# Two quads of modulation weights moved from the S5 stage to the DeltaNet stage, and the low parts of weights made by adding DMA transfers

## The chip, the cores and the metric

One core of a Trainium2 chip runs the whole program. TensorE (PE) multiplies, VectorE (DVE) and ScalarE (ACT) work on elements, SyncE (SP) issues most DMA transfers, and GpSimd (POOL) does almost nothing before the change. The metric is the device time of one execution in microseconds (us).

## The reference, cut to what matters

The program is one inference step of a trunk of two layers on 384 tokens (128 of context, 256 latent) of width 1024, in fp32.

```python
for l in range(2):
    m = silu(cond) @ w_mod[l] + b_mod[l]            # 1024 x 6144: six parts
    sh1, sc1, g1, sh2, sc2, g2 = split(m, 6)
    h = rms(x) * (1 + sc1) + sh1
    out = ab_mix(h) if l == 0 else cd_mix(h)
    x = x + g1 * out
    x = x + g2 * ffn(rms(x) * (1 + sc2) + sh2)
# ab_mix: p = h @ w_in_ab; an S5 state space on one part, gated
#   DeltaNet on the others, both as forward and backward scans; @ w_out_ab
# cd_mix: p = h @ w_in_cd; windowed and differential attention; @ w_out_cd
# ffn:    (silu(conv(h @ up_a)) * (h @ up_b)) @ down
```

## The kernel before, in words

All products are kept near fp32 accuracy by splitting both sides into a high part and a low part, with three matmuls for each pair of tiles: high by low, low by high, high by high (`mm3`, L1119 to L1121, and L1355 to L1357 for the attention layer's projection). Weights come in units of 128x1024 elements (512 KB). `load_unit` (L265) loads one unit into a tile `raw` (three buffers) through SP's DMA queue; ACT rounds it to the high part `wh` (L271), and DVE subtracts that from `raw` to give the low part `wl` (L272). `wh` and `wl` have four buffers each.

The modulation weights `w_mod` are not split. `mod_quad(l, q)` (L987) multiplies two of a layer's six parts: it brings 16 loads of 512 KB straight into tiles that it borrows from the tags `raw`, `wh` and `wl` (SP, L1001), and issues 64 matmuls of 32x512, four at a time on four column groups (L1004), then copies the sums (ACT, L1014), turns them into columns (PE, L1017) and adds the bias (DVE). Quad (0,0) is needed at the very start, (0,1) and (0,2) by the first layer's output projection and feed-forward part, the three quads of layer 1 by the second layer.

The stages of the profiled execution are: setup of norms and S5 tables, until about 86 us; four S5 octets beside the input projection of the first layer (`project`, tiles `pj`, `su`, `sy`, `mm`), until about 222 us; four DeltaNet cores (`gdn_core`, tiles whose names start with g), until about 351 us; the output projection (`out_half`), until 392 us; the feed-forward part, until 681 us; attention (`layer_cd`), until 880 us; the second feed-forward part to the end. In the setup, `s5kd` (L518) stores small S5 tables to DRAM and `s5tp` (L527) reads them back in another layout; the S5 matmuls of line 605 wait for that.

The quads (0,1) and (0,2) run as a side generator: after each unit that `project` multiplies it does one step of a quad, two loads and eight matmuls, with tiles of the tag `raw` alone and a PSUM bank of its own, `mq`. The quads of layer 1 follow the DeltaNet cores 0, 1 and 2, with all eleven buffers and the bank `mod`.

The order in which each engine issues its instructions is not that of the code: a list scheduler (`Order`, with its own table of costs) orders all instructions by their longest path and writes the result to each engine's in-order queue. The hardware then follows these queues.

Of the kernel before, what the change touches and what calls it, by code (L numbers as in the profile page):

```python
# [4 lines left out]

# [1 line left out]

# [209 lines left out]
class Trunk:  # L217
    def __init__(self, ctx, tc, I, O):
        self.ctx, self.tc, self.nc, self.I, self.O = ctx, tc, tc.nc, I, O
        self.tiles = {}  # L220
        nc = self.nc
        self.cp = ctx.enter_context(tc.tile_pool(name="cp", bufs=1))
        self.wp = ctx.enter_context(tc.tile_pool(name="wp", bufs=3))
        self.n = 0
        self.nraw = 0
        self.side = iter(())
        self.cst = self.cp.tile([P, NCST], F32, name="cst")
        self.sml = self.cp.tile([P, NSML], F32, name="sml")
        for tile_, name, first in ((self.sml, "sml", NSML_FIRST), (self.cst, "cst", NCST_FIRST)):
            nc.sync.dma_start(tile_[:, :first], I[name][:, :first])  # L230
            nc.sync.dma_start(tile_[:, first:], I[name][:, first:])
# [31 lines left out]


    def load_unit(self, src, cols=1024):  # L265
        nc = self.nc
        raw = self.t(self.wp, [P, 1024], "raw", bufs=3)
        nc.sync.dma_start(raw[:, :cols], src)
        wh = self.t(self.wp, [P, 1024], "wh", F32R, bufs=4)
        wl = self.t(self.wp, [P, 1024], "wl", F32R, bufs=4)  # L270
        nc.scalar.copy(wh[:, :cols], raw[:, :cols])  # L271
        nc.vector.tensor_sub(wl[:, :cols], raw[:, :cols], wh[:, :cols].bitcast(F32))  # L272
        return wh, wl


# [850 lines left out]
    def project(self, srcs, xh, xl, together=None, tag="mm", n=T):  # L1126


        if together:
            out = [self.bank(tag, [P, n]) for tag in together]  # L1130
            todo = [(p_, *w) for p_, w in zip(out, srcs)]
            for k in range(KD):
                sl = slice(P * k, P * k + P)
                for p_, wh, wl in todo:
                    self.mm3(p_, (wh[:, sl], wl[:, sl]), (xh[k], xl[k]), k == 0, k == KD - 1)
            return out
        out = []
        for src in srcs:
            wh, wl = self.load_unit(src)
            p_ = self.bank(tag, [P, n])  # L1140
            out.append(p_)
            for k in range(KD):
                sl = slice(P * k, P * k + P)
                self.mm3(p_, (wh[:, sl], wl[:, sl]), (xh[k], xl[k]), k == 0, k == KD - 1)
            next(self.side, None)
        return out

    def residual(self, l, gate, n, ps):
# [5 lines left out]

    def ffn(self, l):
        nc, v, t, tc = self.nc, self.nc.vector, self.t, self.tc
        with tc.tile_pool(name=f"fp{l}", bufs=2, reuse_waits="tile") as pool:
            up = [self.I["ffn_up"][l, j, i] for j in range(KF) for i in range(2)]
            pre = self.preload(up[:4])
            hh, hl = self.raw_mod(pool, l, 1)  # L1160
            rb = t(pool, [P, T], "nrb", bufs=1)
            nc.scalar.copy(rb, self.norm_stats(self.np))
            gh, gl = [], []
            cw = self.s("fcw").rearrange("p (l f k) -> p l f k", l=2, k=3)
            cb = self.s("fcb").rearrange("p (l f) -> p l f", l=2)
            first = self.project(pre, hh, hl, together=["mm"] * 4, n=T + 2)
            for j in range(KF):
                pab = first[2 * j:2 * j + 2] if j < 2 else self.project(up[2 * j:2 * j + 2], hh, hl, n=T + 2)
                z = []
                for i, ps in enumerate(pab):  # L1170
                    sh = t(pool, [P, 2], f"fsh{i}")
                    nc.scalar.copy(sh, ps[:, T:])
                    z.append((t(pool, [P, T], f"fz{i}"), sh))
                    v.tensor_mul(z[i][0], ps[:, 0:T], rb)  # L1174
                (pa, sa), (pb, sb) = z
                for c, a, b in SEGS:
                    nc.scalar.activation(pa[:, a:b], pa[:, a:b], AF.Identity, bias=sa[:, c:c + 1])  # L1177
                w = cw[:, l, j]
                y = t(pool, [P, T], "fy")
                nc.scalar.activation(y, pa, AF.Identity, scale=w[:, 1:2], bias=cb[:, l, j:j + 1])  # L1180
                for _, a, b in SEGS:
                    v.scalar_tensor_tensor(y[:, a + 1:b], pa[:, a:b - 1], w[:, 0:1], y[:, a + 1:b],  # L1182
                                           ALU.mult, ALU.add)
                    v.scalar_tensor_tensor(y[:, a:b - 1], pa[:, a + 1:b], w[:, 2:3], y[:, a:b - 1],
                                           ALU.mult, ALU.add)
                s = t(pool, [P, T], "fs")
                nc.scalar.activation(s, y, AF.Silu)  # L1187
                for c, a, b in SEGS:
                    v.scalar_tensor_tensor(s[:, a:b], pb[:, a:b], sb[:, c:c + 1], s[:, a:b], ALU.add, ALU.mult)  # L1189
                a_, b_ = t(pool, [P, T], "fgh", F32R, bufs=KF), t(pool, [P, T], "fgl", F32R, bufs=KF)  # L1190
                nc.scalar.copy(a_, s)
                v.tensor_sub(b_, s, a_.bitcast(F32))
                gh.append(a_)
                gl.append(b_)
            for n in range(KD):
                ps = self.mm([P, T])
                k = 0
                for at in range(0, KF, 8):
                    cnt = min(8, KF - at)
                    wh, wl = self.load_unit(self.I["ffn_down"][l, n][:, at * P:(at + cnt) * P], cols=cnt * P)  # L1200
                    for i in range(cnt):
                        sl = slice(P * i, P * i + P)
                        self.mm3(ps, (wh[:, sl], wl[:, sl]), (gh[k], gl[k]), k == 0, k == KF - 1)
                        k += 1
                self.residual(l, 5, n, ps)


    def layer_ab(self):
        nc, v, t, tc, I = self.nc, self.nc.vector, self.t, self.tc, self.I
        uT, heads = [], []  # L1210
        with ExitStack() as outer:
            sk = outer.enter_context(tc.tile_pool(name="sk", bufs=1, side="right"))
            with self.banks("ps0", mm=2, pj=2, su=1, sy=1, mod=1, mq=1), \
                    tc.tile_pool(name="sp", bufs=1, reuse_waits="tile") as sp:
                with tc.tile_pool(name="st", bufs=1, reuse_waits="tile") as st:
                    self.load_x(st)
# [10 lines left out]
                with tc.tile_pool(name="sw", bufs=1, reuse_waits="tile") as sw:  # L1227
# [2 lines left out]
                        nc.scalar.copy(u, ps)  # L1230
                        uT.append(u)
                    U = [self.s5_inputs(sw, u) for u in uT]
                    self.side = chain(*(self.mod_quad(0, q, tags=("raw",), bank="mq") for q in (1, 2)))
                    for o in range(4):
                        self.s5_octet(sw, o, uT[o], U[o], R[o])
                        if o + 2 < 4:
# [5 lines left out]
                        if o < 3:  # L1242
                            heads.append(self.gdn_head(kq, sw, o, hh, hl, "pj", "gth"))
                    self.s5_states(sw)
                    for _ in self.side:
                        pass
            self.load_x(self.ctx.enter_context(tc.tile_pool(name="xp", bufs=1, reuse_waits="tile")))
            with self.banks("ps1", g1=2, g2=1, g3=2, g4=2, mod=1), \
                    tc.tile_pool(name="gp", bufs=1, reuse_waits="tile") as gp:
                self.gdn_setup(gp)  # L1250
                heads.append(self.gdn_head(kq, gp, 3, hh, hl, "mod", "gcv"))
                self.gelu2(gp, uT[3], "go", 1)
                self.s5_gate(gp, uT)
                ya = [self.split(u, 0.25) for u in uT]
                for h in range(4):
                    self.gdn_core(gp, h, *heads[h])
                    if h < 3:
                        list(self.mod_quad(1, h))
                self.out_half(0, I["w_out_ab"], 0, ya, ("mod",))
                self.out_half(0, I["w_out_ab"], 1, [self.split(x[3]) for x in heads], AB_BANKS)  # L1260

# [67 lines left out]


    def layer_cd(self):
        nc, v, t, tc, I = self.nc, self.nc.vector, self.t, self.tc, self.I
        ident = self.c("ident")
        with tc.tile_pool(name="dpl", bufs=1, reuse_waits="tile") as pool:
# [267 lines left out]

STARTED, BEHIND, WAITED = -1, 0, 1
DMA_RATE, DMA_FIXED = 350.0, 2000.0
PE_GHZ, PE_TICK, PE_WARM = 2.4, 4096 / 1.2, 1210.0


class Order:
# [156 lines left out]
    def duration(self, k):  # L1765
        inst, e = self.insts[k], self.engine[k]
        if self.dma[k]:
            return 450.0
        size = lambda a: math.prod(tuple(x)[1] for x in list(a.bass_ap.ap)[1:])
        outs, ins = ([a for a in ops if hasattr(a, "bass_ap")] for ops in (inst.outs, inst.ins))  # L1770
        if e == "pe":
# [12 lines left out]
    def latency(self, a, b, kind):  # L1784
        if "pools" in (self.engine[a], self.engine[b]):
            return 0.0
        if self.dma[a]:
            return DMA_FIXED + self.bytes[a] / DMA_RATE
        return 0.0 if kind == BEHIND else LATENCY.get((self.engine[a], self.engine[b]), 100)

    def paths(self):
# [27 lines left out]
    def schedule(self):  # L1819
# [12 lines left out]
        def place(k, s):  # L1832
# [17 lines left out]
            if self.dma[k]:  # L1850
                dma_end = max(s + 1500, dma_end) + self.bytes[k] / DMA_RATE
            for b, kind in self.succ[k]:
                f = s + 1 if kind == STARTED else dma_end + 500 if self.dma[k] else end + self.latency(k, b, kind)
                when[b] = max(when[b], f)
                left[b] -= 1
                if not left[b]:
# [78 lines left out]
```

## Time and profile before

| what | value |
|---|---|
| median of 3 runs | 1180.38 us (1179.24 to 1181.22) |
| profiled execution | 1175.78 us, of which the trace spans 1174.0 us |
| mean granted clock of PE | 0.974 |
| PE busy | 1118.2 us (95%) |
| DVE busy | 831.2 us (71%) |
| ACT busy | 582.5 us (50%) |
| DMA moved | 160.85 MB, mean 137 GB/s |

A busy share is a mean over stages with different limits. The profiled execution is 4.6 us under the median; sums are made against it.

### The profile page before, as it was taken

How to read it: one execution, taken by the hardware profiler on the slowest of the kernel's cores; microseconds unless marked ns; L12 is line 12 of the kernel's file. 1: busy time of each engine (PE TensorE's matmuls, PEld its weight loads, DVE VectorE, ACT ScalarE, POOL GpSimd, SP SyncE). 2: the span in 40 equal slices, each digit the busy share in tenths (PEclk: the TensorE clock that was granted, in tenths of full speed). 3: DMA queues.
4: the chain of work that ended last, by engine and by line, in shares of the span. 5: the costliest groups of instructions: out<-in, count | busy, mean ns of one | idle time of the engine just before them, and what ended most of it. 6: DMA issues, size and time to landing. Idle time of an engine off the chain costs nothing.

```text
span 1174.0 us, 20291 instructions
## 1 busy us (share of the span) xinstructions
PE 1118.2 (95%) x7699; PEld 970.2 (83%) x7699; DVE 831.2 (71%) x2097; ACT 582.5 (50%) x1301; POOL 2.9 (0%) x15
## 2 busy tenths in 40 slices
PE   4899999999999999999999979999998999999998
PEld 1587676786559999999999968556788999999998
DVE  7987798689777877777744378786867877676432
ACT  5667463557554555555533234545445655554221
POOL 0000000000000000000000000000000000000000
PEclk9699998999999999999999989999999999999999
DMA  9344474428953234334344323212013343333541
GB/s 372 138 127 149 147 245 164 174 91 301 337 197 127 90 112 140 114 120 143 104 130 130 122 100 125 81 55 81 30 44 115 119 130 122 126 124 103 161 134 55
DMA packets 50737, 160.85 MB, mean 137 GB/s; under 512 B 8272, under 2 KB 12240, under 8 KB 50384
## 3 DMA queue, kind: packets, MB, share of 16 engines
q1 hardware_dynamic: 49200, 154.72, 39.5%
q10 hardware_dynamic: 1440, 4.85, 1.1%
q8 instruction: 60, 0.98, 0.3%
q14 instruction: 37, 0.30, 0.1%
HBM read 156.53 MB, written 3.01 MB: 136 GB/s over the span
## 4 chain that ended last, share of the span: by engine, by line
PE 85%; DVE 8%; DMA 2%; ACT 2%; issue 1%; ACTq 0%; DVEq 0%; SPq 0%
PE mm L1120 16%; PE mm L1121 16%; PE mm L1119 16%; PE mod L1004 3%; PE mm L1355 2%; PE mm L1356 2%; PE mm L1357 2%; PE sc L1477 1%; DVE wl L272 1%; PE mod L1119 1%; PE pj L1121 1%; PE mod L1120 1%; PE mq L1004 1%; PE pj L1120 1%; PE pj L1119 1%
## 5 line engine op out<-in xcount | busy, mean ns | idle before, releaser
L272 DVE TENSOR_TENSOR wl<-raw,wh 128x1024 fp32r<-128x1024 f32 (+2 forms) x193 | 227.0, 1194 | 118.1 <-ACT wh L271 117.8
L271 ACT CAST wh<-raw 128x1024 fp32r<-128x1024 f32 (+2 forms) x193 | 194.0, 1026 | 232.3 <-PE mm L1121 166.6
L1119 PE MATMUL mm<-ah,wl 128*128 128x386 f32 (+1 forms) x732 | 234.8, 343 | 5.2 <-DVE xt L1151 3.6
L1120 PE MATMUL mm<-al,wh 128*128 128x386 f32 (+1 forms) x732 | 233.9, 342 | 2.1 <-DVE al L1097 1.6
L1121 PE MATMUL mm<-ah,wh 128*128 128x386 f32 (+1 forms) x732 | 233.6, 341 | 0.0
L1119 PEld LDWEIGHTS mm<-ah,wl 128*128 128x128 f32 x732 | 138.2, 191 | 6.9 <-ACT wh L271 3.0
L1120 PEld LDWEIGHTS mm<-al,wh 128*128 128x128 f32 x732 | 138.5, 191 | 3.0 <-DVE al L1097 2.1
L1121 PEld LDWEIGHTS mm<-ah,wh 128*128 128x128 f32 x732 | 138.5, 191 | 0.0
L1121 PE MATMUL mm<-fgh,wh 128*128 128x384 f32 x352 | 107.2, 339 | 0.0
L1120 PE MATMUL mm<-fgl,wh 128*128 128x384 f32 x352 | 106.9, 338 | 0.0
L1119 PE MATMUL mm<-fgh,wl 128*128 128x384 f32 x352 | 106.9, 338 | 0.0
L1177 ACT ACTIVATE fz<-fz,fsh 128x128 f32<-128x128 f32 x88 | 35.5, 448 | 67.2 <-DVE fz L1174 67.2
L1119 PEld LDWEIGHTS mm<-fgh,wl 128*128 128x128 f32 x352 | 65.4, 188 | 0.0
L1120 PEld LDWEIGHTS mm<-fgl,wh 128*128 128x128 f32 x352 | 65.2, 188 | 0.0
L1121 PEld LDWEIGHTS mm<-fgh,wh 128*128 128x128 f32 x352 | 65.1, 188 | 0.0
L1151 DVE SCALAR_TENSOR_TENSOR xt<-mm,mod,xt 128x128 f32<-128x128 f32 (+1 forms) x38 | 14.0, 412 | 62.5 <-PE mm L1121 62.5
L1174 DVE TENSOR_TENSOR fz<-mm,nrb 128x384 f32<-128x384 f32 x88 | 45.9, 549 | 0.2
L1182 DVE SCALAR_TENSOR_TENSOR fy<-fz,sml,fy 128x127 f32<-128x127 f32 x88 | 36.4, 413 | 12.8 <-ACT fy L1180 12.1
L1119 PE MATMUL pj<-ah,wl 128*128 128x384 f32 x112 | 39.4, 353 | 2.3 <-DVE wl L272 2.3
L1189 DVE SCALAR_TENSOR_TENSOR fs<-fz,fsh,fs 128x128 f32<-128x128 f32 x88 | 32.7, 413 | 12.4 <-ACT fs L1187 11.2
L1355 PE MATMUL mm<-wh,al 128*128 128x512 f32 (+1 forms) x120 | 38.8, 396 | 2.0 <-DVE al L1074 2.0
L1121 PE MATMUL pj<-ah,wh 128*128 128x384 f32 x112 | 39.9, 356 | 0.0
(661 smaller groups left out, 2163.5 us busy)
## 6 DMA issues: line engine op xcount, KB each, us to landing
raw<-in_ffn_up_dram SPq DMA_DIRECT2D x88, 512.0 KB, 3.4
raw<-in_w_mod_dram SPq DMA_DIRECT2D x54, 512.0 KB, 4.6
raw<-in_ffn_down_dram SPq DMA_DIRECT2D x32, 512.0 KB, 4.5
wh<-in_w_mod_dram SPq DMA_DIRECT2D x21, 512.0 KB, 6.3
wl<-in_w_mod_dram SPq DMA_DIRECT2D x21, 512.0 KB, 6.1
raw<-in_w_in_ab_dram SPq DMA_DIRECT2D x20, 512.0 KB, 3.6
raw<-in_w_in_cd_dram SPq DMA_DIRECT2D x18, 512.0 KB, 3.3
raw<-in_ffn_down_dram SPq DMA_DIRECT2D x16, 384.0 KB, 3.2
```

Of the source, the lines that this page charges most:

```text
L271: nc.scalar.copy(wh[:, :cols], raw[:, :cols])
L272: nc.vector.tensor_sub(wl[:, :cols], raw[:, :cols], wh[:, :cols].bitcast(F32))
L1004: nc.tensor.matmul(pr[32 * n:32 * n + 32], self.sc[:, k, 30 - 2 * b:62 - 2 * b], raws[n // 2][:, 512 * (n % 2):512 * (n % 2) + 512], start ...
L1119: nc.tensor.matmul(out, wl, xh, start=first, stop=False)
L1120: nc.tensor.matmul(out, wh, xl, start=False, stop=False)
L1121: nc.tensor.matmul(out, wh, xh, start=False, stop=last)
L1174: v.tensor_mul(z[i][0], ps[:, 0:T], rb)
L1177: nc.scalar.activation(pa[:, a:b], pa[:, a:b], AF.Identity, bias=sa[:, c:c + 1])
L1182: v.scalar_tensor_tensor(y[:, a + 1:b], pa[:, a:b - 1], w[:, 0:1], y[:, a + 1:b], ALU.mult, ALU.add)
L1189: v.scalar_tensor_tensor(s[:, a:b], pb[:, a:b], sb[:, c:c + 1], s[:, a:b], ALU.add, ALU.mult)
L1355: nc.tensor.matmul(ps[c], hl[k][:, ts_], wh[:, sl], start=k == 0, stop=False)
L1356: nc.tensor.matmul(ps[c], hh[k][:, ts_], wl[:, sl], start=False, stop=False)
```

## The change

The quads (0,1) and (0,2) leave the S5 stage. After core 0 of the DeltaNet stage come quads (0,1) and (0,2), after core 1 quads (1,0) and (1,1), after core 2 quad (1,2). The bank of `mq` goes to `su`.

Outside the feed-forward parts `load_unit` makes the low part in another way: ACT writes the rounded and negated unit into `wl`, and a DMA transfer issued by POOL reads the same unit once more from DRAM and adds it onto `wl`. That holds for 57 units (20 of `w_in_ab` and a small one of `w_ab`, 2 of `w_glu`, 8 of `w_out_ab`, 18 of `w_in_cd`, 8 of `w_out_cd`). The units of both feed-forward parts keep the subtraction on DVE. The scheduler gets a latency and an issue cost for the adding transfers.

```diff
     def load_unit(self, src, cols=1024):
...
         nc.scalar.copy(wh[:, :cols], raw[:, :cols])
-        nc.vector.tensor_sub(wl[:, :cols], raw[:, :cols], wh[:, :cols].bitcast(F32))
+        if self.added:
+            nc.scalar.mul(wl[:, :cols], raw[:, :cols], -1.0)
+            nc.gpsimd.dma_start(out=wl[:, :cols], in_=src, accum_op=ALU.add)
+        else:
+            nc.vector.tensor_sub(wl[:, :cols], raw[:, :cols], wh[:, :cols].bitcast(F32))
         return wh, wl
...
-            next(self.side, None)
...
     def ffn(self, l):
+        self.added = False
...
-            with self.banks("ps0", mm=2, pj=2, su=1, sy=1, mod=1, mq=1), \
+            with self.banks("ps0", mm=2, pj=2, su=2, sy=1, mod=1), \
...
-                    self.side = chain(*(self.mod_quad(0, q, tags=("raw",), bank="mq") for q in (1, 2)))
...
                 for h in range(4):
                     self.gdn_core(gp, h, *heads[h])
-                    if h < 3:
-                        list(self.mod_quad(1, h))
+                    for l, q in ((0, 1), (0, 2), (1, 0), (1, 1), (1, 2))[2 * h:2 * h + 2]:
+                        list(self.mod_quad(l, q))
...
     def layer_cd(self):
+        self.added = True
...
+ADD_MORE = 4500.0
...
-            return 450.0
+            return 900.0 if e == "pool" else 450.0
...
-            return DMA_FIXED + self.bytes[a] / DMA_RATE
+            return DMA_FIXED + self.bytes[a] / DMA_RATE + (ADD_MORE if self.engine[a] == "pool" else 0.0)
```

On SP's queue, at the end of the setup, the kernel before has this order (`in_w_mod` are the quads' loads, `s5kd` and `s5tp` the S5 tables):

```order
L518 DMA s5kd_364<-s5ka_567 64x112 x2
L1001 DMA raw_1371<-in_w_mod_dram 128x1024
L1001 DMA raw_1372<-in_w_mod_dram 128x1024
L527 DMA s5tp_365<-s5kd_364 16x16x64 x2
L268 DMA raw_1379<-in_w_in_ab_dram 128x1024
L527 DMA s5tp_365<-s5kd_364 16x16x64 x6
L1001 DMA raw_1410<-in_w_mod_dram 128x1024
```

At the same place the change has:

```order
L523 DMA s5kd_364<-s5ka_567 64x112
L269 DMA raw_1344<-in_w_in_ab_dram 128x1024
L523 DMA s5kd_364<-s5ka_567 64x112
L532 DMA s5tp_365<-s5kd_364 16x16x64 x8
L269 DMA raw_1376<-in_w_in_ab_dram 128x1024
L269 DMA raw_1408<-in_w_in_ab_dram 128x1024
```

The eight reads of `s5tp` stand in one piece with no load of a quad ahead of them, and from here to the loads of `w_glu` only units of `w_in_ab` follow; the 80 loads of the five quads stand behind `w_glu`.

On POOL's queue, at the start of the S5 stage, the kernel before has only clearings (`s5U` are the inputs of the S5 matmuls, one for each octet):

```order
L379 MEMSET s5Br_308 128x1024
L380 MEMSET s5Bi_309 128x1024
L983 MEMSET msc_72 128x496
L545 MEMSET s5U_930 128x4x2
L546 MEMSET s5U_930 128x4
```

The change has at that place:

```order
L275 DMA wl_728<-in_w_in_ab_dram 128x1024
L275 DMA wl_1231<-in_w_ab_dram 128x128
L275 DMA wl_1347<-in_w_in_ab_dram 128x1024
L550 MEMSET s5U_934 128x4x2
L551 MEMSET s5U_934 128x4
```

The clearings of `s5U` now stand behind the first six adding transfers.

On ACT's queue, where the attention layer begins (`nsq` are the squares of its first norm, `cck` to `cdv` loads of the caches), the kernel before has:

```order
L271 CAST wh_7768<-raw_7766 128x1024
L1035 ACTIVATE nsq_7813<-xt_2551 128x384
L271 CAST wh_7774<-raw_7772 128x1024
L1035 ACTIVATE nsq_7817<-xt_2551 128x384
L271 CAST wh_7780<-raw_7778 128x1024
L1340 DMA cck_7919<-in_cck_dram 128x128
```

The change has:

```order
L274 ACTIVATE wl_7800<-raw_7797 128x1024
L272 CAST wh_7799<-raw_7797 128x1024
L1040 ACTIVATE nsq_7848<-xt_2422 128x384
L274 ACTIVATE wl_7807<-raw_7804 128x1024
L1040 ACTIVATE nsq_7852<-xt_2422 128x384
L274 ACTIVATE wl_7814<-raw_7811 128x1024
L272 CAST wh_7806<-raw_7804 128x1024
L272 CAST wh_7813<-raw_7811 128x1024
L274 ACTIVATE wl_7821<-raw_7818 128x1024
```

Each unit now has two passes on ACT, the negation first; DVE's four subtractions among the norm's small steps are gone.

## Rows read from the trace of the kernel before

**Rows 1.** The page: busy time by engine; chain that ended last.

```profile
PE 1118.2 (95%) x7699; PEld 970.2 (83%) x7699; DVE 831.2 (71%) x2097; ACT 582.5 (50%) x1301; POOL 2.9 (0%) x15
...
PE 85%; DVE 8%; DMA 2%; ACT 2%; issue 1%; ACTq 0%; DVEq 0%; SPq 0%
```

**Rows 2.** Windows: from:to, length, busy PE, PEld, DVE, ACT, POOL; clock, DMA, GB/s.

```profile
50.00:75.00 25.00, 21.41 (x136) 19.09 (x134) 24.48 (x59) 19.96 (x47) 0.37 (x8) 0.80 0.17 51
75.00:100.00 25.00, 22.83 (x217) 17.86 (x217) 20.85 (x43) 14.08 (x47) 0.00 (x0) 1.00 0.63 191
...
150.00:175.00 25.00, 24.85 (x307) 18.09 (x300) 22.73 (x62) 14.21 (x31) 0.00 (x0) 1.00 0.68 233
```

**Rows 3.** Chain of work, 25 to 90 us: start, length, what.

```profile
52.79 1.14 DVE wl L272
...
58.62 1.13 DVE wl L272
...
65.72 1.13 DVE wl L272
...
76.64 5.80 DMA s5tp<-s5kd
...
82.46 4.09 DMA s5tp<-s5kd
```

**Rows 4.** Chain of work, 160 to 205 us.

```profile
168.26 1.21 DVE wl L272
...
169.50 4.71 DMA raw<-in_w_in_ab_dram
...
174.23 1.05 ACT wh L271
...
178.57 0.90 PE su L625 x4
```

**Rows 5.** Windows behind that, and at the stage's end.

```profile
175.00:180.00 5.00, 2.68 (x28) 1.58 (x27) 4.33 (x5) 4.96 (x16) 0.00 (x0) 0.76 0.57 205
180.00:185.00 5.00, 5.00 (x72) 3.26 (x72) 4.74 (x10) 2.10 (x5) 0.00 (x0) 0.55 0.42 128
...
220.00:225.00 5.00, 4.26 (x23) 3.50 (x23) 2.96 (x9) 4.43 (x11) 0.00 (x0) 0.70 0.69 251
```

**Rows 6.** Waits of SP's queue, 60 to 260 us: us, times, longest.

```profile
SPq L1001 <- PE mq L1004: 43.5, 15, 9.5
```

**Rows 7.** Chain of work, 160 to 205 us: one group of a quad's matmuls.

```profile
164.31 1.00 PE mq L1004 x8
```

**Rows 8.** Instructions on the tiles mq and mod: ns min/median/max, first and last start.

```profile
L1017 PE MATMUL mq<-cst,mrow x16: 256/256/277, 152.4 to 220.1; 128*128 128x8 f32 x16
...
L1004 PE MATMUL mod<-raw,msc x64: 592/604/617, 273.0 to 346.8; 128*32 128x512 f32 x64
```

**Rows 9.** The page: groups of instructions.

```profile
L272 DVE TENSOR_TENSOR wl<-raw,wh 128x1024 fp32r<-128x1024 f32 (+2 forms) x193 | 227.0, 1194 | 118.1 <-ACT wh L271 117.8
L271 ACT CAST wh<-raw 128x1024 fp32r<-128x1024 f32 (+2 forms) x193 | 194.0, 1026 | 232.3 <-PE mm L1121 166.6
```

**Rows 10.** DMA issues: out<-in, queue, count, KB each, us to landing.

```profile
wh<-in_w_mod_dram SPq DMA_DIRECT2D x21, 512.0 KB, 6.3
...
raw<-in_w_out_cd_dram SPq DMA_DIRECT2D x8, 512.0 KB, 3.2
```

**Rows 11.** Windows in the DeltaNet stage.

```profile
276.00:284.00 8.00, 8.00 (x63) 4.97 (x55) 7.04 (x40) 7.30 (x21) 0.00 (x0) 1.00 0.97 339
...
316.00:324.00 8.00, 8.00 (x168) 5.57 (x166) 4.86 (x25) 3.84 (x13) 0.00 (x0) 1.00 1.00 349
```

**Rows 12.** Chain of work, 676 to 700 us.

```profile
684.26 4.35 DMA raw<-in_w_in_cd_dram
...
689.79 1.22 DVE wl L272
```

**Rows 13.** Waits, 680 to 700 us.

```profile
PE pt L1052 <- DVE lmp L304: 4.3, 1, 4.3
```

More of the change, by code (lines that the diff above doesn't have):

```diff
@@ L3 @@
 from contextlib import ExitStack, contextmanager
-from itertools import chain
 import numpy as np
@@ L225, in __init__ @@
         self.nraw = 0
-        self.side = iter(())
+        self.added = True
         self.cst = self.cp.tile([P, NCST], F32, name="cst")
@@ L1244, in layer_ab @@
                     self.s5_states(sw)
-                    for _ in self.side:
-                        pass
             self.load_x(self.ctx.enter_context(tc.tile_pool(name="xp", bufs=1, reuse_waits="tile")))
@@ L1331, in layer_cd @@
     def layer_cd(self):
+        self.added = True
         nc, v, t, tc, I = self.nc, self.nc.vector, self.t, self.tc, self.I
@@ L1852, in place @@
             for b, kind in self.succ[k]:
-                f = s + 1 if kind == STARTED else dma_end + 500 if self.dma[k] else end + self.latency(k, b, kind)
+                landed = dma_end + 500 + (ADD_MORE if e == "pool" else 0.0)
+                f = s + 1 if kind == STARTED else landed if self.dma[k] else end + self.latency(k, b, kind)
                 when[b] = max(when[b], f)
```

## The prediction

> **What bounds the kernel now.** I read the page first. TensorE is busy for 1118.2 us of a span of 1174.0, and the chain that ended last runs 85% on PE, 8% on DVE, 2% on DMA [rows 1]. So the change can win at most what PE does not do at full clock: 55.8 us of idle time, and the stretches in which the clock was granted below full. The change takes no matmul away, so every term below is idle time or clock of PE that goes or comes, and I look for these stretch by stretch.
>
> The windows come next [rows 2]. In the setup (50 to 75 us) PE is busy for 21.4 of 25 us at a clock of 0.80, beside a DVE that is full (24.5 of 25); from 75 to 100 it is busy for 22.8. In the S5 stage PE is nearly full (24.9 of 25 in 150 to 175), with a hole at 175 to 180, where it works 2.7 of 5 us, and behind the hole a clock of 0.76 and then 0.55 [rows 5]. In the DeltaNet stage PE is busy in all 8 of 8 us while the DMA engines are full, at 339 and 349 GB/s [rows 11]. The chain of waits tells what stands behind the holes. In the setup it is DVE, with three subtractions of low parts of 1.13 us each on it, and then the reads of `s5tp` (5.80 and 4.09 us) [rows 3]. At 168 us it is a subtraction of 1.21 us on DVE, behind it the load of a unit of `w_in_ab` of 4.71 us, the rounding on ACT, and more ACT work until a PE matmul starts at 178.57 [rows 4]. That load is late because SP's in-order queue stands at the quads' loads: it waits 43.5 us in 15 pieces for matmuls of `mq` to free a tile `raw` [rows 6].
>
> **The change, part by part.**
>
> Moved quads. On the chain a group of eight quad matmuls takes 1.00 us [rows 7], a quad has eight groups, and its 16 small matmuls of 0.256 us run in about 1 us for a quad, half hidden [rows 8]: 9 us a quad, 18 us for two. They leave the S5 stage and come back in the DeltaNet stage, where PE is full [rows 11]. Sum: 0. What counts is what they drag along, at both ends.
>
> At the S5 end the loads of the quads leave SP's queue, and with them the late load of 168 us. The hole gives 2.3 us of idle time, and the clock behind it 5.00 times 0.45 = 2.3 and 2.68 times 0.24 = 0.6 us; the stretch from 220 to 225 adds 4.26 times 0.30 = 1.3 and 0.7 idle [rows 5]. Together 7.2 us, the upper bound; the lower bound is 0, if the scans of the octet leave the same hole for another reason. The quads' matmuls were also filler between the octets' scans, and ACT gets a second pass for each of the 20 units. I take −5 for the hole and the clock, and +1.5 for lost filler and ACT (0 to +5).
>
> At the DeltaNet end 80 loads of 512 KB (41.9 MB) go through the stage in place of 48. At the mean of 344 GB/s of the two full windows [rows 11] that is 122 us. The stage lasted 129 us (222 to 351) and grows by 18 to 147. If the loads start with the stage, 122 fits into 147. In the kernel before the first quad's matmul came at 273.0 us [rows 8], 51 us into the stage; less 6 us for a landing [rows 10] its loads began 45 us in, and 45 + 122 = 167 would be 20 us too long. The bounds are 0 and +20. In the change's order the loads stand right behind those of `w_glu`, so the truth is near the lower bound, but little slack is left for uneven pieces, and I take +3.
>
> Low parts in the setup. The three subtractions leave DVE's chain, 3.4 us, and `s5tp` no longer stands behind two loads of a quad, which is worth up to the 5.80 us of its first read [rows 3]. But PE has only 3.6 + 2.2 us of idle time there [rows 2], so the upper bound of the gain is 5.8 us. Against it stands ACT: four negations, each taken like the rounding's 1.03 us [rows 9], on top of 19.96 of 25 us busy [rows 2], make 24.1 of 25. The lower bound is a loss of 1, if ACT becomes what DVE was. I take −3. The clearings of `s5U` now stand behind six adding transfers on POOL. The sixth waits for PE to free a slot, and PE has other units' matmuls meanwhile, so I cost it at nothing; uncovered it would be one landing.
>
> The price of an adding transfer. No row shows one. Below it is bounded by a plain load on an idle machine, 3.2 us, and above by twice a plain load under full traffic, 2 times 6.3 = 12.6 [rows 10], since it reads the unit and also what it adds onto. I take the middle, an estimate of 8 us, because the stages where it is used are not full of traffic but it has two reads. With the negation a low part is then ready 9 us after its slot is free, where the subtraction took 1.2 [rows 9]. A unit of 24 matmuls of 0.34 us keeps PE for 8.1 us, and there are four slots, so in the steady state 9 us are covered three times over. Not covered are the places where slots are held until late: the first units of `w_out_ab`, whose tiles the last quad holds, and the first of `w_in_cd`, whose tiles the feed-forward part holds. For `w_out_ab` I take +1.5 (0 at 3.2, +10 at 12.6, where several of the eight units come a few us late one after the other).
>
> The attention layer's start. One subtraction of 1.22 us on the chain goes, behind a load of 4.35 [rows 12], and PE waits 4.3 us there for DVE's small steps, between which four subtractions were placed [rows 13]. The gain is at most about 5; if the adding transfer is late it is a loss of about 4, since low parts are then ready after the norm. I take −2.
>
> In the rest of these two stages (30 units) the subtraction was off the path, since the chain there is PE; DVE loses 57 times 1.19 = 68 us of work and ACT gains 58 [rows 9], both at nothing.
>
> The sum: −5 + 1.5 + 3 − 3 + 1.5 − 2 = −4.0 us, from 1175.8 to 1171.8 for an execution like the profiled one. The median stood 4.6 us above it, so I expect 1176.4 us.
>
> **The rivals.**
>
> One: the DeltaNet stage becomes bound by DMA. For it: 122 us of transfers in 147, at rates already full [rows 11], and the adding transfers of `w_out_ab` come on top at the stage's end. Against it: eleven buffers and a queue that has nothing else. It decides once the loads begin more than 25 us into the stage. With 38 us, for example, it costs 13 in place of 3, and the time is about 1187.
> The Trainium skill ("DMA: Bandwidth & Descriptors", section "Issuing engines are not separate DMA queues") says that transfers of different engines share the same DMA engines, so a transfer issued by POOL takes its share from SP's. No row here shows the two together; it would speak for this rival.
>
> Two: the adding transfers land at 12 us or more. Then `w_out_ab` costs 10 in place of 1.5, the attention layer's start +4 in place of −2, and a tight unit or two of the S5 stage 3: −4.0 + 17.5 = +13.5, about 1194. For it: DVE is 71% busy [rows 1] and the transfers queue in order on POOL. Against it: the four slots.
> The Trainium skill ("SBUF — State Buffer", section "Who interferes with whom", and the box on DVE blocking DMA on that page) says that POOL writes such a transfer's descriptors itself, and is locked out while DVE runs certain copies. It would make this rival likelier where DVE is full; no run here shows it yet.
>
> Three: the larger gain. The S5 stage gives back all 7.2 with no loss of filler, the setup 5.8, the start of attention 4.3, and nothing is paid: −17, about 1163.
>
> Four: it doesn't do what it says. The hole at 175 us stays, since ACT's steps and the scans behind it make it, or the freed slots are held by PE anyway. Then −5 falls away, and the time is about 1181.
>
> **How the numbers follow.** The forecast (1172 to 1179) gets 0.37, rival one 0.14, two 0.14, three 0.14, four 0.21. A measurement here can tell about 0.2% (2.4 us) from no change, so faster means under 1178.0 and slower above 1182.8. Faster gets 0.33 of the forecast and 0.14 of rival three, 0.47. Same gets 0.04 of the forecast and 0.15 of rival four, and some of the mildest case of rival one, 0.21 in all; slower gets the other 0.32. The likeliest case's own range is 1172 to 1179. The range must take in rival three nearly whole and most of one and two: 1163 to 1192.
>
> **What would show it.** In the profile after, the load that ended the hole at 168 us should be gone from the chain, the S5 stage should end near 200 us, and its clock be 0.95 or more behind 175. PE should wait for quad loads in the DeltaNet stage by 3 us in all; if 10 or more, rival one is right. The landings of the `wl` transfers by POOL should be near 8 us; at 12 and with PE waits on `wl` in `w_out_ab` and `w_in_cd`, rival two. In the setup no `wl` should stand on the chain, and ACT should be near 24 of 25 us from 50 to 75. The prediction is wrong if the S5 stage without filler leaves PE idle for more than it was before.

## The result, and the profile after

The changed kernel takes 1188.46 us (median of 11 runs, 1186.37 to 1193.58), the kernel before 1181.57 us beside it (11 runs, 1179.24 to 1188.15). The ratio is 1.0066, with a 95% interval of 1.0048 to 1.0084: slower by some 8 us by the ratio, where the forecast was 4 us faster. The profiled execution of the change took 1190.08 us.

The page of the changed kernel, busy time by engine, and the chain that ended last:

```profile
PE 1130.2 (95%) x7699; PEld 979.1 (82%) x7699; DVE 777.3 (65%) x2040; ACT 634.3 (53%) x1358; POOL 52.2 (4%) x72
...
PE 85%; DVE 8%; ACT 4%; DMA 3%; issue 1%; ACTq 0%; DVEq 0%
```

Beside [rows 1], DVE lost 54 us of work and ACT gained 52, somewhat less than the 68 and 58 worked out. But PE is busy for 12 us more with the same 7699 records of matmuls, and ACT has doubled its share of the chain. The windows that answer to [rows 2], one for the place of the hole, and two that are new:

```profile
50.00:75.00 25.00, 19.34 (x119) 16.62 (x119) 21.61 (x59) 23.17 (x58) 3.46 (x4) 0.70 0.62 135
75.00:100.00 25.00, 24.41 (x309) 21.49 (x308) 17.33 (x37) 19.50 (x55) 2.97 (x11) 1.00 0.73 181
150.00:175.00 25.00, 24.61 (x304) 20.88 (x303) 22.37 (x47) 16.58 (x40) 2.59 (x3) 1.00 0.66 164
175.00:200.00 25.00, 24.53 (x236) 19.42 (x237) 17.64 (x36) 12.70 (x30) 1.73 (x2) 1.00 0.36 86
...
355.00:360.00 5.00, 3.17 (x11) 2.61 (x12) 3.76 (x18) 3.75 (x7) 1.72 (x2) 0.53 0.93 201
360.00:365.00 5.00, 2.36 (x10) 2.06 (x9) 0.00 (x0) 4.02 (x11) 0.86 (x1) 0.50 1.02 240
```

The setup gains nothing that these windows show, and other traces agree (see below). From 50 to 100 us PE is idle for 6.2 us, against 5.8 before, and the granted clock of the first window fell from 0.80 to 0.70. The first matmul on `s5tp` does run at 80.7 us in place of 85.6, but that is no measure of progress: the order has changed, and by 81 us PE has started 23 matmuls on `pj` where it had started 51. The hole at 175 us [rows 5] is gone, and the clock from 175 to 200 is 1.00. In its place PE works 5.5 of 10 us at 355 to 365, at a granted clock of 0.53 and 0.50, the lower level, where nothing of the kind stood before. The chain of the change shows what stands there, and a stop of the same kind at `w_glu`, at 202 us:

```profile
202.32 7.62 DMA raw<-in_w_glu_dram
...
210.05 1.06 ACT wl L274
211.10 0.38 ACT gqT L714
...
211.52 0.44 PE mod L1124
...
351.79 2.80 DMA raw<-in_w_out_ab_dram
354.61 4.48 DMA raw<-in_w_out_ab_dram
...
360.98 0.19 ACT wl L274
...
361.95 0.35 ACT gvn L814
...
363.11 0.79 PE g L821 x2
```

ACT's queue is in order. A negation (`wl`, L274) stands in it and waits for its unit to land; behind it stands a small copy (`gqT`, `gvn`) of a DeltaNet step, for which PE waits. PE's waits, 200 to 230 us and then 351 to 372 us (in total, times, longest):

```profile
PE mod L1124 <- ACT gqT L714: 1.0, 1, 1.0
...
PE g L821 <- ACT gvn L814: 3.7, 2, 2.6
```

The DMA issues of the change, which answer to [rows 10]:

```profile
raw<-in_w_in_cd_dram SPq DMA_DIRECT2D x18, 512.0 KB, 6.0
...
wl<-in_w_in_cd_dram POOLq DMA_DIRECT2D x18, 512.0 KB, 6.7
...
wl<-in_w_out_ab_dram POOLq DMA_DIRECT2D x8, 512.0 KB, 6.8
```

The adding transfers land in 6.4 to 7.0 us (9.5 for `w_glu`, where the quads' loads run), so the estimate of 8 was near. What it did not hold is that the plain loads beside them got slower: the unit of `w_in_cd` lands in 6.0 us, against 3.3 before. (e3 below has adding transfers for the attention layer alone: there `w_in_cd` lands in 6.1 us, and `w_in_ab` in 3.5, against 3.6 before.)

By stages, the change is 20 us behind at the last residual of the output projection (418.1 against 398.0 us). The attention layer gives 5 us back (from the first norm step to its last residual 190.6 against 195.2). These two executions differ by 14 us, more than the medians do: the profiled one of before was shorter than any of its 11 timed runs. Differences of a few us in the first layer are therefore taken from ratios, not from one pair of traces.

### The profile page after: what moved, and what is told of

It is laid out like the page before. It is cut to its first block, busy times and chain, and to the rows that moved or that the text cites. A ratio compares the mean times of both kernels' runs of the same rounds, so it can differ in the third digit from the quotient of the medians.

```text
span 1188.3 us, 20449 instructions
## 1 busy us (share of the span) xinstructions
PE 1130.2 (95%) x7699; PEld 979.1 (82%) x7699; DVE 777.3 (65%) x2040; ACT 634.3 (53%) x1358; POOL 52.2 (4%) x72
## 4 chain that ended last, share of the span: by engine, by line
PE 85%; DVE 8%; ACT 4%; DMA 3%; issue 1%; ACTq 0%; DVEq 0%
PE mm L1125 16%; PE mm L1126 16%; PE mm L1124 16%; PE mod L1009 4%; PE mm L1358 2%; PE mm L1360 2%; PE mm L1359 2%; PE sc L1480 1%; PE pj L1124 1%; PE mm L1540 1%; PE pj L1125 1%; PE pj L1126 1%; DVE xt L1155 1%; PE mod L1124 1%; ACT wl L274 1%
## 5 line engine op out<-in xcount | busy, mean ns | idle before, releaser
L277 DVE TENSOR_TENSOR wl<-raw,wh 128x1024 fp32r<-128x1024 f32 (+1 forms) x136 | 158.9, 1191 | 103.9 <-ACT wh L272 103.8
L274 ACT ACTIVATE wl<-raw 128x1024 fp32r<-128x1024 f32 (+1 forms) x57 | 59.2, 1042 | 45.6 <-PE mm L1359 23.8
L1009 PE MATMUL mod<-raw,msc 128*32 128x512 f32 x128 | 36.5, 654 | 11.3 <-DMA raw<-in_w_mod_dram 11.3
```

The costliest lines, as they stand in the source:

```text
L274: nc.scalar.mul(wl[:, :cols], raw[:, :cols], -1.0)
L1009: nc.tensor.matmul(pr[32 * n:32 * n + 32], self.sc[:, k, 30 - 2 * b:62 - 2 * b], raws[n // 2][:, 512 * (n % 2):512 * (n % 2) + 512], start ...
```

## The experiments

Two theories stood at first. A: the adding transfers in the first layer cost the time, where ACT stands at negations; the moved quads are worth something. B: the moved quads cost it, in a DeltaNet stage that is full of transfers. Four kernels part the change: quads moved or not, and adding transfers everywhere, in the attention layer alone, or nowhere.

**e1: the quads alone.**

```diff
-        if self.added:
+        if False:
```

Expected: 

> The quads are moved, all low parts stay on DVE. Theory A (the adding transfers in the first layer cost the time: ACT's in-order queue stands at a negation until a late unit lands, with copies of the recurrences behind it; moving the quads is itself worth the hole at 175 us): 0.995 to 1.000 of before, 3 to 6 us faster at best, S5 stage about 20 us shorter, DeltaNet stage about 19 us longer, no stop of 7 us at the last quad. Theory B (the DeltaNet stage with 80 quad loads is bound by DMA, and that costs the time): 1.005 to 1.010, as the whole change.

Measured: 1185.26 us, ratio 1.0045 (1.0025 to 1.0065). Slower, just under B's range: half of A falls. The moved quads lose 5 us by themselves (together with the bank of `mq` that goes to `su`; no run has the one without the other).

**e2: the adding transfers alone**, with the quads beside the S5 octets as before (the side generator and its bank put back).

Expected: 

> The quads stay beside the S5 octets as before; the 57 low parts outside the feed-forward parts are made by adding transfers. Theory A: 1.002 to 1.008, with ACT standing at negations in the first layer, and a gain of about 5 us in the attention layer against it. Theory B: 0.996 to 1.000, only the attention layer's gain shows.

Measured: 1189.98 us, ratio 1.0070 (1.0045 to 1.0095). Half of B falls too: the transfers lose without the quads' help. The two losses don't add: e1 and e2 would make 1.0115 together, and the change is at 1.0066. In e2 PE waits 5.7 us, in 7 pieces, for loads of the quads beside the octets, where the change has no such wait.

**e3: adding transfers in the attention layer alone**, the rest as before.

```diff
-        self.added = True
+        self.added = False
...
     def layer_cd(self):
         self.added = True
```

Expected: 

> The quads stay as before; only the 26 units of the attention layer are made by adding transfers. Both theories take the attention layer's gain from the traces, about 5 us from the first norm to the second feed-forward part: 0.995 to 0.998. If it is 1.000 or more, the gain seen in the trace of the change was a difference between two executions.

Measured: 1172.31 us, ratio 0.9931 (0.9906 to 0.9955). It wins 8 us, more than expected. The windows of the attention stage, before and then in e3, show where:

```profile
680.00:892.00 212.00, 196.26 (x996) 145.75 (x995) 166.93 (x546) 103.83 (x249) 0.00 (x0) 0.96 0.24 79
```

```profile
688.00:890.00 202.00, 191.38 (x995) 143.48 (x994) 139.22 (x519) 126.49 (x274) 21.61 (x25) 0.97 0.61 145
```

DVE loses 28 us of work in a stage where it was busy for 79%, and 10 us of the stage go. PE's waits that end with a DVE step fall from 15 to 8 us there; ACT has room for 23 us more. In its first layer e3 runs the same instructions in the same order as before on PE, DVE, ACT and SP; there the two profiled executions still differ by 8 us (last residual at 406.0 against 398.0). That is the size of the scatter from one execution to another.

**e4: quads moved, adding transfers in the attention layer alone.**

Expected: 

> The change with the 31 units of the first layer back on DVE; the quads are moved and the attention layer's low parts are made by adding transfers. Theory A: 0.990 to 0.996, the best of the four. Theory B: 1.002 to 1.006, since the quads' cost stays.

Measured: 1178.15 us, ratio 0.9990 (0.9977 to 1.0004), between the ranges of the two theories. Against e1 the attention layer again wins 6.5 us; against e3 the quads again lose, 7 us.

The next three put single groups of units back on DVE, in the change. Theory A, cut down: the cost is where a negation waits for a late unit. Theory C: the cost is spread over all units.

**e5: `w_out_ab` on DVE; e7: `w_glu` and `w_out_ab` on DVE** (the second line stands ahead of the gate in e7).

```diff
+                self.added = False
                 self.out_half(0, I["w_out_ab"], 0, ya, ("mod",))
```

Expected of e5: 

> The change with the eight units of w_out_ab back on DVE; the projection, w_glu and the attention layer keep adding transfers. Theory A (the adding transfers cost where ACT's in-order queue stands at a negation for a late unit of w_out_ab, with copies of the last DeltaNet core behind it): output projection as in the run with adding transfers in attention alone, 8 to 10 us less than the whole change, 0.998 to 1.001 of before. Theory C (the cost is spread over the projection's units, ACT's second pass and the doubled reads): at most 3 us less, 1.004 or more.

Expected of e7: 

> The change with w_glu and w_out_ab back on DVE; in the first layer only the 21 units of the projection are made by adding transfers. Theory A: the stop of 7.6 us at w_glu goes too, 0.995 to 0.999. Theory C: 1.002 or more.

Measured: e5 1180.74 us, ratio 1.0013 (0.9995 to 1.0030); e7 1174.39 us, ratio 0.9953 (0.9934 to 0.9972). C falls; e5 lies just above A's range, e7 in it. The ten units of `w_glu` and `w_out_ab` cost 11.3 thousandths, some 13 us, and the projection's units win: e7 against e4 is 0.9953 against 0.9990. In the trace of e7 neither unit stands on the chain ahead of `gqT` or `gvn`. At `w_glu`, from 200 to 215 us, PE works 14.4 us in e7 and 11.0 in e5: about half of what its two units cost stands at that place, and where the rest goes wasn't separated.

**e6: the negation of `w_out_ab` on DVE in place of ACT**, the transfers kept.

```diff
+            if self.negate:
+                nc.vector.tensor_scalar(wl[:, :cols], raw[:, :cols], -1.0, None, ALU.mult)
+            else:
                 nc.scalar.mul(wl[:, :cols], raw[:, :cols], -1.0)
```

Expected: 

> The change with the negation of the eight units of w_out_ab made by DVE in place of ACT; the adding transfers stay. If ACT's queue is what costs, nearly all of it comes back: 0.998 to 1.002. If the late landing of the adding transfers or the doubled traffic costs, it stays at 1.004 to 1.008, with PE waiting for wl of w_out_ab.

Measured: 1185.38 us, ratio 1.0051 (1.0035 to 1.0068). In the range of the second branch, but not for its reason: little comes back, and PE does not wait for `wl` either. The chain of e6 shows where the wait went:

```profile
351.35 4.74 DMA raw<-in_w_out_ab_dram
...
356.29 0.69 DVE wl L275
...
357.12 0.21 DVE gWt L924
...
359.72 0.20 DVE gTc L928
...
359.97 0.50 PE g L951 x18
```

The late unit now stands on the chain ahead of a negation on DVE, with the DeltaNet steps `gWt` behind it. So it isn't ACT alone. How much of the loss is the wait is less clear than on ACT: DVE is idle for only 0.8 us at the negations, and the four of them, 0.69 us each, stand among the steps of the recurrence.

**e9: negations placed later**, by one number of the scheduler.

```diff
-ADD_MORE = 4500.0
+ADD_MORE = 0.0
```

Expected: 

> The change with one number of the scheduler's table altered: an adding transfer is priced like a plain load (ADD_MORE 0 in place of 4500), so that the longest path through a negation is shorter and negations are placed later on ACT. If the early place of the negations, ahead of the DeltaNet copies gvn and gqT, is what costs: the stops at w_glu and w_out_ab shrink, 0.998 to 1.002. If the transfers' own latency or traffic is the cost, PE then waits for wl of w_out_ab: 1.004 to 1.010.

Measured: 1197.47 us, ratio 1.0133 (1.0104 to 1.0162). Now PE waits for the landing, in the chain of waits of e9:

```profile
382.19 1.06 ACT wl L274
...
383.55 0.85 POOL wl L275
...
393.59 7.71 DMA wl<-in_w_out_ab_dram
...
401.35 1.01 PE g L1124 x2
```

and its waits, 340 to 420 us:

```profile
PE g L1124 <- DMA wl<-in_w_out_ab_dram: 5.1, 2, 3.5
```

So at `w_out_ab` neither place was good: early, an engine stands at the negation; late, PE waits for the transfer. (At `w_glu` no such wait shows in e9. The number moves the negations of all adding transfers, so not all of the loss need stand here.)

**e12: quads in `wh` and `wl` tiles alone**, so that `raw` tiles are free early.

```diff
-                        list(self.mod_quad(l, q))
+                        list(self.mod_quad(l, q, tags=("wh", "wl")))
```

Expected: 

> The change with the quads of the DeltaNet stage loaded into tiles of wh and wl alone (eight in place of eleven), so that the tiles raw are free for w_glu and w_out_ab early. If the late units of w_out_ab (a tile raw held by the last quad) make the stop at 351 us: the units land before, the stop goes, 0.999 to 1.002. If eight tiles are too few for the quads, PE waits for quad loads in the DeltaNet stage: 1.006 or more.

Measured: 1194.92 us, ratio 1.0121 (1.0095 to 1.0147). As the first branch had it, three units of `w_out_ab` land by 223 us, and PE's wait for `gvn` at the stage's end is gone. The time is in the second branch all the same, but PE waited for a quad load for only 0.9 us, so that branch names the wrong cause; the quads themselves took more PE time. That led to the next question. PE's busy time on the quads' matmuls alone, in windows (a quad is 32 matmuls, not 64 as said above, and each has two records): the kernel before with two quads beside the octets and three beside the DeltaNet cores, then the change and e12 with five there:

```profile
80.00:230.00 150.00, 19.49 (x128) 2.96 (x128) 0.97 0.53 175
230.00:400.00 170.00, 32.85 (x192) 4.70 (x192) 1.00 0.58 203
```

```profile
215.00:410.00 195.00, 56.95 (x320) 8.21 (x320) 0.96 0.82 277
```

```profile
205.00:410.00 205.00, 72.54 (x320) 10.18 (x320) 0.99 0.83 273
```

A step of a quad is four matmuls on four column groups that run together. In the written order of the change, 27 runs hold only two of the four, with other work between; in e12, 57. The chain of the change shows both kinds, by records:

```profile
226.69 0.98 PE mod L1009 x4
...
230.85 0.99 PE mod L1009 x8
```

Half a step takes as long as a whole one. The scheduler has a rule that keeps such a group together (`gangs`); it holds in the S5 stage, and breaks in the DeltaNet stage, where the matmuls also depend on a marker for reused memory that has a later number than any instruction.

**e11: whole steps** in the kernel of e7, **e13** in the change, **e14** in the kernel before, **e15** in e3.

```diff
-                if used & held[k] or any(a > g[0] and a not in g for a in self.pred[k]):
+                if used & held[k] or any((len(self.insts) > a or not quad) and a > g[0] and a not in g for a in self.pred[k]):
```

(`quad` is true where the group's first matmul is one of a quad.)

Expected of e11: 

> The kernel with adding transfers in the projection and the attention layer and the quads moved (0.9953 of before), with the scheduler made to keep each step of a quad together: all four column groups in one run. In that kernel 25 of the runs hold half a step. If the half steps are where the quads' 4 us more of PE time in the DeltaNet stage come from: quads 1 to 5 us less busy in the trace, 0.990 to 0.994. If not, 0.995 or more.

Expected of e13: 

> The change as it is, with each step of a quad kept in one run of four column groups. If the splits cost 0.5 us each: 27 of them gone, 0.994 to 0.998, against 1.0066 for the change. If the gain of the run before came from something else there (w_glu and w_out_ab on DVE), 1.003 or more.

Expected of e14: 

> The kernel before, with nothing else altered but that each step of the three quads in the DeltaNet stage is kept in one run. 14 splits of 0.5 us: 0.993 to 0.996. If PE's time there is hidden behind the cores' own chain: 0.998 to 1.002.

Expected of e15: 

> The kernel with adding transfers in the attention layer alone (quads (0,1) and (0,2) beside the S5 octets), with whole steps: 0.987 to 0.990 if the gains add. If moving the two quads is itself worth nothing, this ties with the moved quads with whole steps (0.9862); if moving pays about 6 us once the steps are whole, it stays at 0.989 or above.

Measured: e11 1165.21 us, ratio 0.9862 (0.9836 to 0.9889); e13 1183.81 us, 1.0037 (1.0020 to 1.0054); e14 1180.77 us, 1.0014 (0.9994 to 1.0035); e15 1172.11 us, 0.9935 (0.9912 to 0.9958). The quads' own PE time falls, in e11 by more than the 1 to 5 us that were expected. It was 55.95 us in e7, with 25 half runs, and in e11 it is:

```profile
205.00:410.00 205.00, 43.41 (x320) 6.56 (x320) 0.99 0.72 263
```

12.5 us less, or 0.50 for each half run; e11 is below the range of its first branch. But the time follows only in part: 10.7 us in e11, 3.4 in e13, none in e14 and e15. In e14 the quads of the DeltaNet stage fall from 32.85 to 25.36 us of PE, and PE is idle for it (7.2 of 10 us busy at 350 to 360). The four runs agree with this: with three quads in that stage PE's time is not its bound; with five it is, unless the stops at `w_glu` and `w_out_ab` stand in its way. e13 falls into its second branch: in the change more than half of the loss stays without split steps. With whole steps, the quads moved and the projection's units added to, e11 beats the quads beside the octets (e15) by 0.9862 to 0.9935; no run has the moved quads with whole steps and the attention layer's units alone, so the share of each isn't known.

**e8 and e10: other places for the quads.** e8 is e3 with the quads begun behind the first octet; e10 is e3 with the projection's units made by adding transfers too.

```diff
                     for o in range(4):
+                        if o == 1:
+                            self.side = chain(*(self.mod_quad(0, q, tags=("raw",), bank="mq") for q in (1, 2)))
                         self.s5_octet(sw, o, uT[o], U[o], R[o])
```

Expected of e8: 

> The kernel with adding transfers in the attention layer alone (0.993 of before), with the two quads still beside the S5 octets, but begun behind the first octet, so that no load of a quad stands ahead of the reads of s5tp. If the 6 us that the moved quads win in the setup come from that queue alone: the first matmul of s5tp near 81 us in place of 87, and 0.987 to 0.990. If the later quads crowd the end of the S5 stage as much: 0.992 to 0.996.

Expected of e10: 

> The two quads stay beside the S5 octets; adding transfers for the projection's units and the attention layer, w_glu and w_out_ab on DVE. If the projection's adding transfers win their 4 us by themselves (as they did with the quads moved): 0.988 to 0.991. If they win only where no quad load shares SP's queue: 0.992 to 0.996, as with the attention layer alone.

Measured: e8 1174.99 us, 0.9955 (0.9937 to 0.9973); e10 1180.51 us, 0.9999 (0.9981 to 1.0017). In e8 the reads of `s5tp` do land sooner, from 80.2 to 83.7 us against 82.4 to 86.5 before; yet the first matmul on them runs at 87.4 us, with no idle time of PE ahead of it, since the order puts other matmuls first. So that mark can't tell what the two loads cost, and e8 is no faster than e3. In e10 the projection's units lose 8 us where they won 4 with the quads moved, outside both branches. Its traced first layer is as long as that of e3 (last residual at 405.7 against 406.0), but the trace holds a lead: beside the octets PE waits 4.6 us, in 6 pieces, for the quads' loads, against 0.4 in e3, and the quads' matmuls are busy for 24.65 us against 20.10. So the quads' loads come late beside adding transfers, as in e2; that this makes up the 8 us isn't shown.

## Why the prediction was wrong

The runs e1, e4, e7, e5 and the change form a row in which each adds one part. From their ratios, at 1180 us, each step with an uncertainty of about 3 us:

| part added | ratio after it | us | predicted |
|---|---|---|---|
| quads moved | 1.0045 | +5.3 | −3.5 with the setup |
| attention units | 0.9990 | −6.5 | −2 |
| projection units | 0.9953 | −4.4 | 0 beside the setup |
| `w_glu` | 1.0013 | +7.1 | 0 |
| `w_out_ab` | 1.0066 | +6.3 | +1.5 |

**Moved quads: the step "Sum: 0" failed.** It took a quad as 9 us of PE in either place, from one whole group of eight records [rows 7]. The busy times on these lines are 19.5 us for the two beside the octets, and 24.1 (56.95 − 32.85) beside the DeltaNet cores, because there the order splits steps, and half a step costs a whole one. In e1 the difference is 3.7 us of PE time, in the change 4.6; undoing all splits in the change gave 3.4 us of time (e13). The late load and its hole did go [rows 4, 5], as said. The sign of being wrong, that PE is idle for more without the filler, did not come: from 75 to 200 us it is idle for 4.8 us against 7.9.

**The setup: the term of −3 is not seen.** It counted idle time of PE from 50 to 100 us as if that went with the subtractions and the two loads. ACT is at 23.2 of 25 us, near the 24 that were expected, but PE's idle time is 6.2 us against 5.8, with a lower clock. One pair of traces can't tell 3 us, but the others say the same: four traces with the quads beside the octets (before, e3, e14, e15) have 5.8 to 8.6 us of idle time there, seven with the quads moved (e1, e4, e7, e11, e12, e13 and the change) 5.1 to 7.1. What PE waits for instead wasn't taken apart. With 3.7 us of split steps, this makes up 7 of the 9 us between −3.5 and +5.3, about what the uncertainty allows; but the +3 for uneven loads in the DeltaNet stage didn't come either, so some of the loss stays open.

**`w_out_ab` and `w_glu`: the term of 1.5 failed, and `w_glu` had none.** The landing was estimated well. What was wrong is "ready 9 us after its slot is free": the tile `raw` comes free by the same quads as `wl`, so the unit's own load (4.7 to 7.6 us there) comes ahead of the negation, and the sum, with 1.05 for the negation and 6.8 for the transfer, is 13 to 15 us. The cover was taken too long as well: 0.34 us is the length of one matmul's record, but records overlap, and at full clock a matmul follows the last after 0.17 to 0.18 us:

```profile
213.01 0.17 PE mod L1125
213.19 0.17 PE mod L1126
```

So a unit of 24 keeps PE for 4.2 us and three units for 12.6, which covers 9 us once and not three times over. And the wait for the load stands in an engine's in-order queue with the recurrence behind it. Rival two had the place and the sign, but named the landing at 12 us; it was 6.8. e6 and e9 show for `w_out_ab` that neither another engine nor a later place cures it; e5 and e7 that the subtraction, with a path shorter by the transfer, does.

**The attention layer was undersized.** The term looked at the start alone (one subtraction on the chain, [rows 12, 13]). That start came out near the forecast: PE's waits for DVE ahead of the first product fall from 7.6 to 5.2 us in e3. What failed is the sentence that put the other units at nothing, as off the path: in the rest of the stage, where DVE was busy for 79%, PE's waits for DVE fall by some 5 us more. In all it is 10 us between the two traces, 6.5 to 8 by the ratios.

**The projection: a gain that was costed at nothing** but in the setup. It is there only with the quads moved (e7 against e4), and gone with them in place (e10). Why it wins wasn't taken apart.

**Rival one** (DMA as the bound of the DeltaNet stage) did not decide: PE waited for quad loads for under 1 us in e12, with 8 tiles in place of 11, and none of the change's PE waits there names a quad load. The Trainium skill's rule that transfers of all engines share the DMA engines ("DMA: Bandwidth & Descriptors", section "Issuing engines are not separate DMA queues") agrees with the plain loads that land in 6.0 in place of 3.3 us. The Trainium skill's warning that a transfer issued by POOL can be held up while DVE runs certain operations ("SBUF — State Buffer", section "Who interferes with whom") is not seen here: 6.9 us in the attention layer of e3, with DVE busy for 69% of it. No run varies what DVE runs beside the transfers, so none tests it.

The best version is that of e11: quads moved with whole steps, adding transfers for the projection and the attention layer, subtractions at `w_glu`, `w_out_ab` and in the feed-forward parts. It runs in 1165.21 us, 0.9862 of the kernel before.

## What to carry to other kernels

A change of several parts that nets to little can hold large gains and losses: this one held 11 us of gain and 19 of loss, and a kernel for each part showed which to keep. When a step is made longer to relieve an engine (here 1.2 us on DVE become 8 or more through a transfer), ask for each place when its inputs arrive and its buffer comes free, and what stands behind it in the queue of the engine that now waits. When work that fills the array by groups is moved, look at the written order: a group that is split costs its full time twice. And when the order changes, the time of one matmul is no mark of progress: count what has been done by then.

## What the runs showed that was not expected

A run of two matmuls of 32x512 on two column groups takes as long as four on four groups (0.98 against 0.99 us); by 25 such runs in e7 and none in e11 that is 0.50 us of PE for each. A transfer that adds 512 KB onto a tile lands in 6.4 to 7.0 us, and POOL is busy for 0.86 us to issue it. A matmul's record of 0.34 us does not mean that PE is taken for so long: the next one starts after 0.17 to 0.18 us. One and the same order of instructions took 318 and 312 us from the first `s5tp` matmul to the last residual of the output projection in two executions (e3 and before).
